# A hybrid decoder block in split fp32: reciprocal square roots seeded by ScalarE, output weights split where they are used, convolution sums kept in PSUM

## The chip, the core and the metric

One core of a Trainium2 chip runs the whole block. Its engines are TensorE (PE, matrix products), VectorE (DVE), ScalarE (ACT) and GpSimd (POOL); the SyncE queue (SP) issues most transfers. Each engine works off its own instructions strictly in order. The metric is the device time of one execution in microseconds, as a median over runs. The time also has a part before the first and after the last instruction; the span is what lies between those two.

## The reference

One layer, 1024 tokens, width 1024, 16 learned meta tokens put in front and cut off at the end; everything in fp32. With `rms` for a root-mean-square norm and `ln` for a layer norm it computes:

```
h   = concat(meta, x)                          # 1040 tokens
p   = rms(h, g_pre) @ w_in                     # 1024 x 2560: b, c, h, v, g (512 each)
y_a = b * conv3(c * h_)                        # causal depthwise, 3 taps
z   = conv31(v * sigmoid(g)) + bias            # causal depthwise, 31 taps
y   = concat(y_a, silu(ln(z)))                 # 512 + 512
h   = h + rms(y @ w_out, g_post)               # 1024 x 1024
f   = (silu(n @ w_gate) * (n @ w_up)) @ w_down # n = rms(h, g_ffn), inner width 2816
out = (h + rms(f, g_out))[16:]
```

Each `rms` and `ln` holds a reciprocal square root, of one number per token.

## The kernel before

**Split products.** Every fp32 operand of a product is kept as two rounded parts, hi and lo: a cast on ACT gives hi, a subtraction on DVE or GpSimd gives lo. `mm3` (L109 to L111) then issues three matmuls, hi\*hi, hi\*lo, lo\*hi, into one PSUM tile. That is why each product has three lines in the profile.

**Order.** Nothing is scheduled by a planner: the kernel is built with a manual schedule, and the order of the Python calls is the order of each engine's queue. An instruction that must wait holds up everything behind it on its engine.

**Stage 1, input projection.** The 2560 output columns are 20 *units* of 128: `g`, `v` (gate and value of the long convolution), `c`, `h`, `b` (short convolution), four of each. The units g0 and v0 are computed while x arrives. Then PE transposes and spreads the norm factors: `ss_x` (sums of squares, L271), `rsqrt_n` on DVE, `pb_x` (L286, in `start_g`) and ACT copies to `rB` (L289). Then 18 units follow in the order of `UNITS`: g1 v1 g2 v2 g3 v3, then c, h, b for each of the four column groups. While unit i is multiplied, `split_unit` prepares the weights of unit i+1 (hi on ACT, lo on GpSimd, L155), and `after[...]` deals with the result of unit i-1. `LEAD_IN` and `AT` say which convolution taps and which layer-norm steps are issued at which unit; `AT[(14, 1)]` is `ln_mean`, whose matmuls `pm` (L435) need all taps done.

**The long convolution.** The tokens are held in even and odd halves e and o. Three short convolutions give both outputs: a common one on o with summed weights (`ac`, 16 taps), one on d = e - o (`ae`, 16 taps) and one on e[1:] - o (`ao`, 15 taps). Each tap is one DVE instruction over 512 columns (L341). The accumulators lie in PSUM, but the first tap of each takes its start value from z in SBUF, and the common result goes back to z. The differences d and e[1:] - o are DVE instructions (L352, L353). For three of the four groups (of 128 channels) the first eight common taps are done on ACT and GpSimd (L335, L336), since `HEAD` is (1, 8, 8, 8).

**Output weights.** `pre_out` (called around the start of stage 1) loads each of 8 blocks of w_out, splits it (ACT L256, DVE L257) and writes hi and lo to DRAM. In stage 2 `next_o` loads hi and lo back from there on the GpSimd queue (L740), 18 times 512 KB each.

**Stage 2, output projection.** Token rows of 128 are taken in three groups, (0,1,2), (3,4,5), (6,7); `group` multiplies all 8 weight blocks for the rows of the group (`po`), `norms` makes the two norms, `turn` transposes the normed rows (`pt`) into the operands of the next stage.

**Stage 3, gate and up.** Seven products for each pair of column blocks (a Strassen form), 11 pairs; x and y are the PSUM tiles, B11, B21, T1, T2, ... the token-side operands, `op` the weight-side ones. `a_side` makes a weight-side operand, `split_lo` and `copy_hi` a token-side one.

**Stage 4, down projection.** Seven products again (qx, qy), with final norms row by row at the end of the program; L966 writes the output rows.

**`rsqrt_n`** (L113 to L132): on DVE alone. It forms v, makes a first guess with integer arithmetic on the bits of v (two instructions) and makes three Newton steps.

Of the kernel before, what the change touches and what calls it, by code (L numbers as in the profile page):

```python
# [15 lines left out]
P = 128  # L16
# [18 lines left out]
MAGIC = 1597463007.0  # L35
RSCALE = -1.0 / 8192.0
# [21 lines left out]
def hybrid_block(ctx: ExitStack, tc: tile.TileContext, xT, x, w_in, w_out, w_gate, w_up, w_down, par, g_post, g_ffn, g_out, out):  # L58
# [35 lines left out]
    pr = const.tile([P, lines(NPAR)], F32, name="pr")[:, :NPAR]  # L94
# [18 lines left out]
    def rsqrt_n(ss, inv_n, eps, n, name, more=None):  # L113

        v = sm.tile([P, 16], F32, tag="v", name=f"v_{name}")
        b = sm.tile([P, 16], I32, tag="b", name=f"b_{name}")
        s = sm.tile([P, 16], F32, tag="s", name=f"s_{name}")
        t = sm.tile([P, 16], F32, tag="tt", name=f"t_{name}")
        v, b, s, t = v[:, :n], b[:, :n], s[:, :n], t[:, :n]
        nc.vector.tensor_scalar(v, ss, inv_n, eps, op0=ALU.mult, op1=ALU.add)  # L120
        if more is not None:
            nc.vector.tensor_scalar(v, more, inv_n, v, op0=ALU.mult, op1=ALU.add)
        nc.vector.tensor_scalar(b, v.bitcast(I32), 1, None, op0=ALU.logical_shift_right)
        nc.vector.tensor_scalar(s.bitcast(I32), b, -1.0, MAGIC, op0=ALU.mult, op1=ALU.add)
        for k in (3.0, 12.0, 768.0):
            if n == 1:
                nc.vector.tensor_scalar(t, s, v, s, op0=ALU.mult, op1=ALU.mult)
            else:
                nc.vector.tensor_tensor(t, s, s, op=ALU.mult)
                nc.vector.tensor_tensor(t, t, v, op=ALU.mult)  # L130
            nc.vector.scalar_tensor_tensor(s, t, k, s, op0=ALU.subtract, op1=ALU.mult)
        return s  # L132


    nc.scalar.dma_start(pr, par)
    xhb = [xa.tile([P, 2 * TT], F32R, tag="x", name=f"xh{j}").rearrange("p (a b) -> p a b", a=2) for j in range(4)]
# [3 lines left out]
    wo = [dram.tile([P, 2, D], F32R, tag=f"wo{k}", name=f"wo{k}") for k in range(KD)]  # L140
# [88 lines left out]
    split_unit(UNITS[0])  # L229
    nc.vector.tensor_tensor(sa[0], sa[0], sa[1], op=ALU.add)  # L230

# [13 lines left out]
    ws_o = {}  # L245

    def load_raw_o(k):
        if k < KD:
            ws_o[k] = yap.tile([P, D], F32, tag="y", name=f"ws_o{k}")
            nc.sync.dma_start(ws_o[k], w_out[k])  # L250

    def pre_out(k):
        load_raw_o(k + 2)
        ws = ws_o.pop(k)
        h, l = (yap.tile([P, D], F32R, tag="y", name=f"{c}_o{k}") for c in ("wh", "wl"))
        nc.scalar.copy(h, ws)  # L256
# [18 lines left out]
    rx = rsqrt_n(sx[:, : NT + 1], 512.0 / D, RMS_EPS, NT + 1, "x")  # L275
    rB = row(gp, "rB", "rB", TT, bufs=1)
# [51 lines left out]
    def conv_head(a):  # L328

        ze, zo = halves_of(a)  # L330
        o = gpad[a][1]
        nc.scalar.activation(zo, o[:, :HALF], AF.Identity, scale=wc(a, 0), bias=pr[:, O_CBB + a : O_CBB + a + 1])
        for i in range(1, HEAD[a]):
            t = ct.tile([P, HALF], F32, tag="ct", name=f"ct{a}{i}")
            nc.scalar.activation(t, o[:, i : i + HALF], AF.Copy, scale=wc(a, i))  # L335
            nc.gpsimd.tensor_tensor(zo, zo, t, op=ALU.add)  # L336

    def taps(name, src, w, first, n, init, out):
        acc = aux.tile([P, 512], F32, tag="a", name=name)
        for i in range(first, n):  # L340
            nc.vector.scalar_tensor_tensor(out if i == n - 1 else acc, src[:, i : i + HALF], w(i), init if i == first else acc, op0=ALU.mult, op1=ALU.add)  # L341
            yield

    def common(a):
        ze, zo = halves_of(a)
        yield from taps(f"ac{a}", gpad[a][1], lambda i: wc(a, i), HEAD[a], NE, zo, zo)

    def even(a):
        e, o = gpad[a]
        ze, zo = halves_of(a)  # L350
        d = ct.tile([P, (G0 + TT) // 2], F32, tag="d", name=f"d{a}")
        nc.vector.tensor_tensor(d, e, o, op=ALU.subtract)  # L352
        nc.vector.tensor_tensor(o[:, :-1], e[:, 1:], o[:, :-1], op=ALU.subtract)  # L353
# [54 lines left out]
    def after_b(a):  # L408
# [4 lines left out]
        nc.scalar.copy(yh[a], cv[a])  # L413
        nc.vector.tensor_tensor(yl[a], cv[a], yh[a].bitcast(F32), op=ALU.subtract)
# [8 lines left out]
    def sums(srcs, outs):  # L423
        for q in range(3):
            for hf in range(2):
                nc.vector.tensor_tensor(outs[hf], srcs(hf, 0) if q == 0 else outs[hf], srcs(hf, q + 1), op=ALU.add)
# [787 lines left out]
```

## Time and profile before

| | |
|---|---|
| median of 3 runs | 1059.92 us (1058.63 to 1061.58) |
| the profiled execution | 1059.18 us |
| its span | 1057.2 us |
| mean granted TensorE clock | 0.972 |
| PE busy | 986.2 us, 93% of the span, 4643 matmuls |
| DVE, ACT, POOL busy | 773.9, 378.4, 296.3 us |

In the profile a row of the timeline reads: start, duration, engine, line of the kernel, operation, output from inputs, shape, and in brackets how long the engine was idle before and what released it. A windows row lists for a stretch of time the busy time of each engine with its number of instructions, then the granted clock of TensorE (1.00 is full speed), the busy share of the DMA engines and GB/s. A waits row gives what an engine waited for: in total, how many times, longest.

### The profile page before, as it was taken

What the parts mean: (1) busy time and instruction counts of PE and PEld (TensorE: products, weight loads), DVE (VectorE), ACT (ScalarE), POOL (GpSimd) and SP (SyncE); (2) the same over time, 40 slices, a digit from 0 to 9 for tenths busy, and PEclk for the clock granted to TensorE, in tenths of its full rate; (3) what the DMA queues carried; (4) which work ended last, traced back from release to release, by engine and by line L of the source; (5) the groups of instructions that cost most, each with busy time, mean ns of one, the idle gap of its engine ahead of it and who ended that gap; (6) DMA issues with size and microseconds to landing.
All of it is one profiled execution on the core that took longest, in us unless ns stands there. A gap on an engine that the chain in (4) does not pass through costs nothing.

```text
span 1057.2 us, 12732 instructions
## 1 busy us (share of the span) xinstructions
PE 986.2 (93%) x4643; PEld 839.9 (79%) x4643; DVE 773.9 (73%) x1087; ACT 378.4 (36%) x616; POOL 296.3 (28%) x267
## 2 busy tenths in 40 slices
PE   9599998879999797998999999999999899999994
PEld 8499998769787675876888888888888788888773
DVE  6689999997414558789888888888878343446667
ACT  7433331233413254333443433434334233322331
POOL 0247774443112100026134223313413522212110
PEclk9799998989999999999999999999999999999998
DMA  7851111001759552034634443353324989867765
GB/s 304 301 216 41 41 42 60 20 20 61 254 163 316 183 184 74 1 122 177 219 130 149 160 170 148 130 209 117 142 100 169 384 309 376 270 183 204 268 215 209
DMA packets 64909, 180.80 MB, mean 171 GB/s; under 512 B 6864, under 2 KB 7248, under 8 KB 64848
## 3 DMA queue, kind: packets, MB, share of 16 engines
q1 hardware_dynamic: 43344, 109.40, 28.2%
q0 software_dynamic: 16272, 59.25, 17.4%
q10 hardware_dynamic: 5232, 11.35, 3.0%
q8 instruction: 36, 0.59, 0.2%
q14 instruction: 25, 0.20, 0.1%
HBM read 122.83 MB, written 57.15 MB: 170 GB/s over the span
## 4 chain that ended last, share of the span: by engine, by line
PE 60%; DVE 26%; DMA 5%; ACT 4%; issue 4%; POOL 1%; SPq 0%; DVEq 0%; ACTq 0%; POOLq 0%
PE x L109 6%; PE x L111 6%; PE x L110 6%; PE y L109 5%; PE y L110 5%; PE y L111 5%; DVE ao L341 4%; DVE ae L341 4%; PE qx L110 3%; PE qx L109 3%; PE qx L111 3%; DVE ac L341 3%; PE qy L110 2%; PE qy L111 2%; PE qy L109 2%
## 5 line engine op out<-in xcount | busy, mean ns | idle before, releaser
L592 DVE TENSOR_TENSOR op<-u,op 128x512 fp32r<-128x512 f32 x154 | 142.9, 955 | 61.6 <-ACT op L605 61.6
L605 ACT CAST op<-u 128x512 fp32r<-128x512 f32 x154 | 90.7, 618 | 163.6 <-DVE u L592 153.6
L592 DVE TENSOR_TENSOR db<-wb,db 128x512 fp32r<-128x512 f32 x77 | 53.7, 701 | 93.2 <-ACT db L1015 92.9
L1015 ACT CAST db<-wb 128x512 fp32r<-128x512 f32 x77 | 47.0, 621 | 117.4 <-PE qx L111 55.2
L595 POOL TENSOR_TENSOR C<-C,C 128x512 f32<-128x512 f32 x11 | 15.4, 1400 | 246.8 <-ACT C L705 246.8
L109 PE MATMUL qx<-db,a 128*128 128x512 f32 x176 | 68.7, 390 | 3.2 <-DMA a<-gdA 3.2
L110 PE MATMUL qx<-db,a 128*128 128x512 f32 x176 | 68.7, 390 | 0.4 <-DVE db L592 0.3
L111 PE MATMUL qx<-db,a 128*128 128x512 f32 x176 | 68.5, 389 | 0.0
L595 POOL TENSOR_TENSOR U<-U,U 128x512 f32<-128x512 f32 x22 | 31.2, 1419 | 92.1 <-ACT U L705 83.4
L109 PE MATMUL qy<-db,a 128*128 128x512 f32 x132 | 51.5, 390 | 0.5 <-ACT db L1015 0.5
L110 PE MATMUL qy<-db,a 128*128 128x512 f32 x132 | 51.5, 390 | 0.3 <-DVE db L592 0.3
L111 PE MATMUL qy<-db,a 128*128 128x512 f32 x132 | 51.4, 389 | 0.0
L991 POOL DMA_DIRECT2D a<-gdS x44 | 23.3, 531 | 92.2 <-PE qy L111 47.2
L589 DVE TENSOR_TENSOR U<-y,U 128x512 f32<-128x512 f32 x66 | 42.7, 681 | 7.8 <-PE y L111 7.8
L341 DVE SCALAR_TENSOR_TENSOR ae<-d,pr,ae 128x512 f32<-128x512 f32 x56 | 41.8, 747 | 0.0
L109 PEld LDWEIGHTS qx<-db,a 128*128 128x128 f32 x176 | 33.0, 188 | 10.8 <-ACT U L705 3.6
L109 PE MATMUL y<-T2h,op 128*128 128x512 f32 x88 | 35.5, 403 | 5.6 <-DVE G L595 4.4
L592 DVE TENSOR_TENSOR u<-u,u 128x512 f32<-128x512 f32 x44 | 39.9, 907 | 0.8
L109 PE MATMUL x<-B21h,op 128*128 128x512 f32 x88 | 35.0, 398 | 5.3 <-ACT U L677 5.3
L109 PE MATMUL p_h<-xh,wh_h 128*128 128x342 f32 x96 | 32.8, 341 | 7.3 <-DVE cv L412 7.3
L110 PEld LDWEIGHTS qx<-db,a 128*128 128x128 f32 x176 | 33.0, 188 | 7.9 <-DVE db L592 1.2
L341 DVE SCALAR_TENSOR_TENSOR ao<-g,pr,ao 128x512 f32<-128x512 f32 x52 | 38.8, 747 | 0.0
(290 smaller groups left out, 3015.1 us busy)
## 6 DMA issues: line engine op xcount, KB each, us to landing
a<-gdS POOLq DMA_DIRECT2D x44, 512.0 KB, 4.7
a<-gdA POOLq DMA_DIRECT2D x33, 512.0 KB, 5.8
u<-w_gate_u SPq DMA_DIRECT2D x22, 512.0 KB, 5.4
u<-w_up_u SPq DMA_DIRECT2D x22, 512.0 KB, 5.9
gdS<-HI SPq DMA_DIRECT2D x44, 256.0 KB, 2.3
wh_o<-wo POOLq DMA_DIRECT2D x18, 512.0 KB, 5.8
wl_o<-wo POOLq DMA_DIRECT2D x18, 512.0 KB, 7.2
gdA<-HI SPq DMA_DIRECT2D x33, 256.0 KB, 2.0
```

The source lines that it names most:

```text
L109: nc.tensor.matmul(o, lh, rh, start=start, stop=False, skip_group_check=again)
L110: nc.tensor.matmul(o, lh, rl, start=False, stop=False, skip_group_check=again)
L111: nc.tensor.matmul(o, ll, rh, start=False, stop=stop, skip_group_check=again)
L341: nc.vector.scalar_tensor_tensor(out if i == n - 1 else acc, src[:, i : i + HALF], w(i), init if i == first else acc, op0=ALU.mult, op1=AL ...
L589: (eng or nc.vector).tensor_tensor(o, a, b, op=ALU.add)
L592: (eng or nc.vector).tensor_tensor(o, a, b, op=ALU.subtract)
L595: (eng or nc.vector).tensor_tensor(o, a, b, op=ALU.mult)
L605: nc.scalar.copy(t[:, 0, :], src)
L991: nc.gpsimd.dma_start(loads[n, j], gd[an][j])
L1015: nc.scalar.copy(t[:, 0, :], b)
```

## The change

1. `rsqrt_n` takes its first guess from ScalarE's function Abs_reciprocal_sqrt and makes one Newton step instead of three. ScalarE holds one table of functions at a time; `table(f)` issues a one-column instruction that loads a table ahead of its use. The program now loads seven tables; before it loaded three.
2. `pre_out` is gone. `load_o` loads the raw block of w_out on the SP queue and `split_o` splits it, once for each group of rows except that the blocks used last by one group are used first by the next: 14 loads of 512 KB. The first two blocks are split with GpSimd, the others with DVE. Blocks 3 and 4 are kept between the first groups.
3. In the start, lo of g1 and v1 is made by DVE, not GpSimd; all of v0 is multiplied ahead of `ss_x`; `start_g` is issued after two of the eight blocks of g1 instead of after one.
4. The convolution accumulators stay in PSUM from the first tap on: ACT writes the first common tap (or copies the eight) into PSUM tile `ac`, `ae` starts from `ac`, and the odd taps go on in `ac` itself. The differences are made by GpSimd. `value` writes even and odd tokens contiguously. The schedule of taps is new. The sums for the layer norm are kept in PSUM, and lo of a `b` unit is made three taps later.
5. Before stage 3: the hi half of B21 is made between the reciprocal square root and the residual sum, T2 is split in 128-column pieces, the weight sums of the product s = 4 are made earlier, T4's tiles are taken earlier, and in `a_side` both casts are issued ahead of both subtractions.

```diff
-    def rsqrt_n(ss, inv_n, eps, n, name, more=None):
-        nc.vector.tensor_scalar(v, ss, inv_n, eps, op0=ALU.mult, op1=ALU.add)
...
-        nc.vector.tensor_scalar(b, v.bitcast(I32), 1, None, op0=ALU.logical_shift_right)
-        nc.vector.tensor_scalar(s.bitcast(I32), b, -1.0, MAGIC, op0=ALU.mult, op1=ALU.add)
-        for k in (3.0, 12.0, 768.0):
...
+    def table(f):
+        nc.scalar.activation(eps[:, 2:3], eps[:, 0:1], f)
+
+    def rsqrt_n(ss, inv_n, e, n, name):
...
+        nc.scalar.activation(s, ss, AF.Abs_reciprocal_sqrt, scale=inv_n, bias=at)
+        nc.vector.tensor_scalar(v, ss, inv_n, e, op0=ALU.mult, op1=ALU.add)
...
+        nc.vector.scalar_tensor_tensor(r, t, 3.0, s, op0=ALU.subtract, op1=ALU.mult)
+        return r
...
+    def load_o(k):
+        raw_w["o", k] = wp.tile([P, D], F32, tag="ws", name=f"ws_o{k}")
+        nc.sync.dma_start(raw_w["o", k], w_out[k])
+
+    def split_o(k, eng=None):
...
+        nc.scalar.copy(wu[k][0], raw_w["o", k])
+        (eng or nc.vector).tensor_tensor(wu[k][1], raw_w["o", k], wu[k][0].bitcast(F32), op=ALU.subtract)
...
-    split_unit(UNITS[0])
     nc.vector.tensor_tensor(sa[0], sa[0], sa[1], op=ALU.add)
+    split_unit(UNITS[0], nc.vector)
...
+    mm_k(pu["v", 0], split_w["v", 0], KD - 1, 0, T3, 3)
     NT = SEQ // P
...
-    mm_k(pu["v", 0], split_w["v", 0], KD - 1, 0, T3, 3)
...
+    def differences(a):
+
+        e, o = gpad[a]
+        dd[a] = ct.tile([P, (G0 + TT) // 2], F32, tag="d", name=f"d{a}")
+        nc.gpsimd.tensor_tensor(dd[a], e, o, op=ALU.subtract)
+        nc.gpsimd.tensor_tensor(e[:, 1:], e[:, 1:], o[:, :-1], op=ALU.subtract)
...
+    def conv(a):
...
+        both = aux.tile([P, 512], F32, tag="a", name=f"ac{a}")
+        if HEAD[a] > 1:
+            nc.scalar.copy(both, zo)
+        else:
+            nc.scalar.activation(both, o[:, :HALF], AF.Identity, scale=wc(a, 0), bias=pr[:, O_CBB + a : O_CBB + a + 1])
+        yield from taps(o, lambda i: wc(a, i), HEAD[a], NE, both, both, both)
+        ae = aux.tile([P, 512], F32, tag="a", name=f"ae{a}")
+        yield from by_turns(taps(dd[a], lambda i: wb(a, 2 * i), 0, NE, both, ae, ze), taps(e[:, 1:], lambda i: wb(a, 2 * i + 1), 0, NE - 1, both, both, zo))
...
-    AT = {(0, 1): start_g, (14, 1): ln_mean, (15, 3): ln_var, (15, 7): ln_spread}
+    AT = {(0, 2): start_g, (14, 1): ln_mean, (15, 3): ln_var, (15, 7): ln_spread}
...
-    up, down_ = list(range(KD)), list(range(KD - 1, -1, -1))
+    up, middle = list(range(KD)), [5, 6, 7, 3, 4, 0, 1, 2]
...
-    s1, left = group((0, 1, 2), up, {})
+    s1, left = group((0, 1, 2), up, {0: ahead(3, 5), 1: ahead(4, 6), 2: ahead(5, 7), 3: ahead(6, 0), 4: ahead(7, 1), 6: ahead(None, 2)})
...
-    s1, left = group((3, 4, 5), down_, {4: turns(0, 1), 5: turns(2)})
+    s1, left = group((3, 4, 5), middle, {1: ahead(0, 5), 2: ahead(1, 6), 3: ahead(2, 7), 4: turns(0, 1), 5: turns(2)})
...
-    hn = norms((6, 7), left, s1, hs, between)
+    hn = norms((6, 7), left, s1, hs, between, lambda: copy_hi(X[2], r21))
+    table(AF.Silu)
```

The change moves instructions at three places of which the prediction speaks. The first is DVE's queue at the norm of x, where the convolution begins. The names are: `v_x`, `b_x`, `s_x`, `t_x` the steps of the reciprocal square root, `wl_o` lo of an output weight, `sg` the gate of unit g0, `rB` the spread norm. Before (left out in the middle are the second step of the guess and the nine of the three Newton steps):

```order
L273 COPY sx<-ss_x 128x8
L274 COPY sx<-ss_x 16x1
L120 TENSOR_SCALAR v_x<-sx 128x9
L123 TENSOR_SCALAR b_x<-v_x 128x9
...
L257 TENSOR_TENSOR wl_o_438<-ws_o_358,wh_o_437 128x1024
L257 TENSOR_TENSOR wl_o_446<-ws_o_366,wh_o_445 128x1024
L257 TENSOR_TENSOR wl_o_454<-ws_o_435,wh_o_453 128x1024
L257 TENSOR_TENSOR wl_o_462<-ws_o_443,wh_o_461 128x1024
L477 TENSOR_TENSOR sg_423<-sg_423,rB 128x1044
```

And now:

```order
L241 TENSOR_TENSOR sa_134<-sa_134,sa_135 128x1040
L153 TENSOR_TENSOR wl_g_218<-ws_g_186,wh_g_217 128x1024
L272 COPY sx<-ss_x 128x8
L273 COPY sx<-ss_x 16x1
L124 TENSOR_SCALAR v_x<-sx 128x9
L128 TENSOR_TENSOR tt_x<-s_x 128x9
L129 TENSOR_TENSOR tt_x<-tt_x,v_x 128x9
L130 SCALAR_TENSOR_TENSOR r_x<-tt_x,s_x 128x9
L153 TENSOR_TENSOR wl_v_399<-ws_v_188,wh_v_398 128x1024
L479 TENSOR_TENSOR sg_377<-sg_377,rB 128x1044
```

The chain has four DVE instructions where it had twelve, its guess `s_x` comes from ACT, and the splits of output weights that stood between it and the gate are gone; lo of g1 and of v1 has come to DVE.

The second place is the end of the common taps of the first convolution group on DVE. `ac`, `ae`, `ao` are accumulators in PSUM, `g` holds e and o, `d` is their difference, z lies in SBUF, `pr` and `wsum` are the weights. Before:

```order
L341 SCALAR_TENSOR_TENSOR ac_585<-g_508,wsum,ac_585 128x512 x5
L341 SCALAR_TENSOR_TENSOR z_427<-g_508,wsum,ac_585 128x512
L352 TENSOR_TENSOR d_707<-g_508 128x527
L353 TENSOR_TENSOR g_508<-g_508 128x526
L341 SCALAR_TENSOR_TENSOR ae_710<-d_707,pr,z_427 128x512
L341 SCALAR_TENSOR_TENSOR ao_712<-g_508,pr,z_427 128x512
L341 SCALAR_TENSOR_TENSOR ae_710<-d_707,pr,ae_710 128x512
```

And now:

```order
L344 SCALAR_TENSOR_TENSOR ac_512<-g_442,wsum,ac_512 128x512 x13
L310 TENSOR_TENSOR g_606<-p_v_527,sg_508 128x2x174 x3
L344 SCALAR_TENSOR_TENSOR ac_512<-g_442,wsum,ac_512 128x512 x2
L344 SCALAR_TENSOR_TENSOR ae_616<-d_445,pr,ac_512 128x512
L344 SCALAR_TENSOR_TENSOR ac_512<-g_442,pr,ac_512 128x512
L344 SCALAR_TENSOR_TENSOR ae_616<-d_445,pr,ae_616 128x512
```

The two differences have left DVE, and no tap but the last of each output touches z.

The third place is ACT's queue at the start of the output projection. `yh` and `ybh` are hi parts of the operands, `wh_o` and `w_o` of the weight blocks, `gB_post` and `gB_ffn` gains. Before:

```order
L413 CAST yh_2255<-cv_2193 128x1024
L473 ACTIVATE gB_post<-gB_post 128x1024
L473 ACTIVATE gB_ffn<-gB_ffn 128x1024
L527 CAST ybh_2282<-z_427 128x2x512 x2
L527 CAST ybh_2288<-z_428 128x2x512 x2
```

And now:

```order
L406 CAST yh_2192<-cv_2124 128x1024
L542 CAST ybh_2219<-z_396 128x2x512
L167 CAST wh_o_2223<-ws_o_2190 128x1024
...
L542 CAST ybh_2231<-z_397 128x2x512 x2
L475 ACTIVATE gB_post<-gB_post 128x1024
L475 ACTIVATE gB_ffn<-gB_ffn 128x1024
L117 ACT_TABLE_LOAD
L117 ACTIVATE pr<-pr 128x1
L167 CAST w_o_2217<-ws_o_2227 128x1024
L167 CAST w_o_2218<-ws_o_2325 128x1024
```

Left out is a second `ybh` cast of z_396. The hi cast of block 3 (`w_o_2217`) now stands behind eight instructions that follow `yh` of the last unit.

More of the change, by code (lines that the diff above doesn't have):

```diff
@@ L519, in hybrid_block @@
     ps2 = pa.enter_context(tc.tile_pool(name="ps2", bufs=6, space=PSUM, reuse_waits="tile"))
+    held = [xg.tile([P, 2, D], F32R, tag="x", name=f"w_o{k}") for k in (3, 4)]
     for a in range(4):
@@ L768, in group, with ahead, f @@
         return s1, {i: leave_psum(i, pm[i], s1, q) for q, i in enumerate(grp)}
-    up, down_ = list(range(KD)), list(range(KD - 1, -1, -1))
-    for q in range(3):
-        next_o()
+    def ahead(k=None, n=None):
+        def f():
+            if k is not None:
+                split_o(k)
+            if n is not None:
+                load_o(n)
+        return f
+    up, middle = list(range(KD)), [5, 6, 7, 3, 4, 0, 1, 2]
+    load_o(4)
     hs = {i: residual_x(i) for i in (0, 1, 2)}
     pairs = {j: Pair(j) for j in range(3)}
-    pairs[0].load(0)
-    pairs[1].load(0, (0,))
-    s1, left = group((0, 1, 2), up, {})
+    s1, left = group((0, 1, 2), up, {0: ahead(3, 5), 1: ahead(4, 6), 2: ahead(5, 7), 3: ahead(6, 0), 4: ahead(7, 1), 6: ahead(None, 2)})
     B11 = [blocks(big(f"B11{j}", pool=bp)) for j in "hl"]
-    for q, t in ((0, 0), (1, 1), (0, 1), (1, 0)):
-        raw[q, t] = blocks(big(f"raw{q}{t}", F32))
+    for q in range(2):
+        raw[q, 0] = blocks(big(f"raw{q}0", F32))
     hn = norms((0, 1, 2), left, s1, hs)
@@ L825, in a_side, with pairs_load @@
             pairs[j + 1] = Pair(j + 1)
-        made[s] = [pairs[j].a_side(n, m, places[m] if places else None) for m in range(2)]
+        src = sums.pop(s, None) or [pairs[j].a_side(n, m) for m in range(2)]
+        t = [operand_hi(src[m], f"{n}_{j}{m}", places[m] if places else None) for m in range(2)]
+        for m in range(2):
+            sub(t[m][:, 1, :], src[m], t[m][:, 0, :].bitcast(F32))
+        made[s] = t
+    def pairs_load():
+        split_o(7)
+        pairs[1].load(0, (0,))
     def early():
+        for q in range(2):
+            raw[q, 1] = blocks(big(f"raw{q}1", F32))
         turns(3, 4, 5)()
         pairs[1].load(0, (1,))
-        t1_sum(0)
-        t1_sum(1)
+        for i in range(2):
+            t1_sum(i)
         a_side(0)
@@ L854, in hybrid_block @@
     st = ctx.enter_context(tc.tile_pool(name="st", bufs=11, reuse_waits="tile"))
+    X[6] = pair("T2", (rp, rp))
     a_side(3)
-    for i in range(2):
-        t2_sum(i)
-    def t2():
-        X[6] = pair("T2", (rp, rp))
-        copy_hi(X[6], T2r)
-        split_lo(X[6], T2r)
+    for f in (t2_sum, t2_hi, t2_lo):
+        for i in range(2):
+            f(i)
     def t1():
@@ L914, in hybrid_block @@
             turns(6, 7)()
+            sums[4] = [pairs[0].a_side(6, m) for m in range(2)]
         if s in (14, 15):
```

230 lines of the change are left out of this document (113 added, 117 removed).

## The prediction

> **What bounds the kernel now.** I read the page first, then PE's waits, then the stretches of time one by one, then single rows where two engines meet.
>
> ```profile
> PE 986.2 (93%) x4643; PEld 839.9 (79%) x4643; DVE 773.9 (73%) x1087; ACT 378.4 (36%) x616; POOL 296.3 (28%) x267
> PE pb_x L286 <- ACT rB L289: 10.6, 1, 10.6
> PE p_h L109 <- DVE cv L412: 7.3, 2, 3.9
> PE pm L435 <- DVE zs L426: 6.2, 1, 6.2
> PE x L109 <- ACT U L677: 5.3, 2, 4.1
> PE po L110 <- DMA wl_o<-wo: 3.9, 4, 1.8
> PE po L109 <- DMA wh_o<-wo: 3.5, 1, 3.5
> ```
>
> PE is busy 93% of the span, so a gain can only come from its 71 us of idle time and from the time in which its clock is low. A gain on DVE, ACT or POOL counts only where PE waits for it. The waits are few and long, and lie before 435 us. The windows show stretch by stretch what each engine did (length, then the busy time of PE, its weight loads, DVE, ACT and POOL, then the granted clock, the DMA share and GB/s).
>
> ```profile
> 62.40:119.60 57.20, 57.20 (x361) 57.20 (x360) 53.55 (x66) 19.87 (x25) 39.25 (x24) 1.00 0.17 61
> 119.60:142.10 22.50, 22.50 (x145) 22.50 (x144) 22.40 (x30) 8.46 (x11) 15.30 (x12) 1.00 0.11 38
> 200.00:230.00 30.00, 19.95 (x111) 18.94 (x110) 28.83 (x41) 3.85 (x4) 9.86 (x5) 0.87 0.11 36
> 62.40:279.10 216.70, 203.08 (x1157) 191.80 (x1156) 194.44 (x241) 65.10 (x75) 106.95 (x58) 0.96 0.16 54
> 279.10:386.90 107.80, 97.03 (x433) 77.64 (x432) 46.05 (x93) 34.23 (x68) 16.93 (x32) 0.97 0.69 237
> 386.90:432.70 45.80, 38.07 (x161) 30.19 (x161) 37.05 (x68) 20.76 (x36) 0.00 (x0) 0.93 0.20 69
> 500.00:820.00 320.00, 320.00 (x1413) 265.03 (x1413) 268.96 (x346) 128.53 (x231) 87.72 (x57) 1.00 0.42 153
> ```
>
> From 500 to 820 us PE never stops at full clock: nothing is to be had there. The projection (62 to 279) falls behind only after 142 us, where DVE is full (28.83 of 30) and PE waits for it. The start and the stages from 279 to 433 have waits of their own. The change touches these.
>
> **Part A, the start (−15.9).** PE reaches the end of g1 at 62.33 us.
>
> ```profile
> 31.26 2.08 PE L271 MATMUL ss_x<-ones,sa 128*128 128x1 f32 x18 [1.66 <-DVE sa L230]
> 48.13 1.04 ACT L256 CAST wh_o<-ws_o 128x1024 fp32r<-128x1024 f32 x1 [3.31 <-DMA ws_o<-w_out_u]
> 49.31 1.11 PE L286 MATMUL pb_x<-ident,s_x 128*128 128x128 f32 x4 [10.63 <-ACT rB L289]
> 62.33 0.32 PE L109 MATMUL p_v<-xh,wh_v 128*128 128x348 f32 x1
> ```
>
> The 10.63 us are ACT's: its copy to rB stood behind casts of output weights that waited for their loads. `pre_out` is gone, so are these casts. The last nine matmuls of v0 now come ahead of `ss_x`. Nine at the unit's spacing (57.20 / 360 = 0.159) fill 1.43 of the 1.66 us of waiting; the sum that PE waited for also comes earlier, since the subtraction that GpSimd ran beside it has gone behind it on DVE. From 31.1, then: `ss_x` 2.1, 72 matmuls of g1 11.44, `pb_x` 1.9 with its short wait: 46.4, so −15.9. The norm factors must be ready after two blocks of g1, at 36.0; the shortened chain ends near 35. If the thin matmuls of `ss_x` lower the clock once more, up to 1.5 comes back.
>
> **Part B, the projection (−20.2).** The floor of the 216.7 us: five g and v units 57.2, eight c and h units 22.50 / 2 = 11.25 each, four b units at 48 times 0.23 (14 intervals below) = 11.05, and the layer norm's matmuls.
>
> ```profile
> 275.67 0.39 PE L109 MATMUL p_b<-xh,wh_b 128*128 128x512 f32 x1
> 278.89 0.40 PE L111 MATMUL p_b<-xh,wl_b 128*128 128x512 f32 x1
> 229.35 3.46 PE L435 MATMUL pm<-zs,ones 128*128 128x512 f32 x4 [6.15 <-DVE zs L426]
> L446 PE MATMUL pst<-ones,sq 128*128 128x1 f32 x16 | 1.8, 245 | 0.0
> L454 PE MATMUL pv<-ident,s_ln 128*128 128x128 f32 x8 | 1.1, 279 | 0.1
> ```
>
> `pm` needs about 1.3 less at full clock (an estimate from its slow stretch), so the three are 5.1. Together 57.2 + 90.0 + 44.2 + 5.1 = 196.5. The 20.2 above it are 13.5 of waits (7.3 + 6.2) and 6.7 of slow clock behind them. They vanish if DVE is in time. What DVE loses:
>
> ```profile
> 65.62 2.34 DVE L341 SCALAR_TENSOR_TENSOR ac<-g,wsum,z 128x512 f32<-128x512 f32 x1 [1.85 <-ACT z L332]
> L341 DVE SCALAR_TENSOR_TENSOR ae<-d,pr,z 128x512 f32<-128x512 f32 x4 | 9.3, 2337 | 0.0
> L341 DVE SCALAR_TENSOR_TENSOR ae<-d,pr,ae 128x512 f32<-128x512 f32 x56 | 41.8, 747 | 0.0
> L353 DVE TENSOR_TENSOR g<-g 128x526 f32<-128x526 f32 x4 | 8.9, 2221 | 0.2
> L352 DVE TENSOR_TENSOR d<-g 128x527 f32<-128x527 f32 x4 | 6.9, 1718 | 0.0
> 197.51 2.74 POOL L406 TENSOR_TENSOR cv<-cv,rB 128x1024 f32<-128x1024 f32 x1
> 197.92 2.89 DVE L341 SCALAR_TENSOR_TENSOR ae<-d,pr,z 128x512 f32<-128x512 f32 x1
> ```
>
> A first tap with both inputs in SBUF takes 2337 ns on the mean, one on a PSUM accumulator 747. The last two rows say why: the tap at 197.92 takes 2.89 while GpSimd works beside it. Taps with one input in PSUM are not held up so. So the eight first taps of `ae` and `ao` shrink by 8 times 1.59 = 12.7, and the differences, 15.8, leave DVE. DVE's stretch from the first tap (65.62) to the matmul `pm` (229.35) is 163.7 us; without these 28.5 it is 135.2. It begins 3.2 us after g1's end: the gate of g1, its sigmoid and ACT's first tap come ahead, as they do now. So it begins at 49.6 and ends near 185; I give it 6 either way, for the first taps of `ac`, which are shorter too, and for what GpSimd's new work may hold up. In a projection without waits `pm` is due at 46.4 + 57.2 + 67.5 + 22.1 + 1.4 = 194.6 (five units, six, two and a block of the next). The margin is 4 to 16, so I take the whole 20.2. The other bound is that none of it comes; it is a rival below.
>
> **Part C, output projection (−11.8).** 384 `po` matmuls at 0.2267 (18 intervals below) are 87.0, six rows transposed at 1.1 are 6.6: 93.6 of 107.8.
>
> ```profile
> 599.35 0.39 PE L109 MATMUL x<-B11h,op 128*128 128x512 f32 x1
> 603.43 0.39 PE L109 MATMUL x<-B11h,op 128*128 128x512 f32 x1
> 376.92 1.03 PE L573 MATMUL pt<-ident,hn 128*128 128x128 f32 x8
> 51.07 1.28 ACT L478 ACT_TABLE_LOAD   x1
> ```
>
> The reloads from DRAM (7.4 us of waits) are replaced by half the traffic and by 14 casts on ACT (1.04 in the row at 48.13) and as many subtractions, most on DVE (2.36 for two of this shape in part D), engines that were busy 34 and 46 of 107.8. The tightest is block 3: its cast stands behind eight ACT instructions of about 1.1, a table load of 1.28 and the one behind it; with its own cast that is some 11.3, then 1.2 for lo: 12.5 after the last unit, while PE asks for it after 54 matmuls, at 12.2. I keep 2.4 of stalls (blocks 3 and 5, transposes): 96.0.
>
> The Trainium skill ("ScalarE: Activation LUTs", What ACT_TABLE_LOAD costs) counts a drain with each switch, some 2.7 us in all. That speaks against four more loads. The row at 51.07 shows 1.28. By the page block 3 would be 1.4 later, and the total 1003; no run here yet shows a load with work behind it that PE waits for.
>
> **Part D, start of gate and up (−8.4).** Six products of 24 matmuls 32.6 and two transposed rows 2.2 are 34.8 of 45.8.
>
> ```profile
> 388.72 0.17 DVE L120 TENSOR_SCALAR v_pm<-pm 128x2 f32<-128x2 f32 x1
> 390.90 0.16 DVE L131 SCALAR_TENSOR_TENSOR s_pm<-t_pm,s_pm 128x2 f32<-128x2 f32 x1
> 413.70 2.36 DVE L592 TENSOR_TENSOR T2l<-T2r,T2h 128x1024 fp32r<-128x1024 f32 x2
> ```
>
> One root costs 2.35 on DVE, and two stand on this path; four instructions and ACT's guess come to about 1.1, which saves 2.4. T2, sum and lo, stood last on DVE's list; half of it is now made before the last rows arrive. I leave 2.6 of waits: 37.4. If only the roots help, −2.4.
>
> **Part E, the tail (−2.4).** Two chains of this kind lie behind the last matmul:
>
> ```profile
> 1043.60 0.15 DVE L120 TENSOR_SCALAR v_out<-tot 128x1 f32<-128x1 f32 x1
> 1045.48 0.16 DVE L131 SCALAR_TENSOR_TENSOR s_out<-t_out,s_out 128x1 f32<-128x1 f32 x1
> ```
>
> 2.04 each becomes about 0.85, bounds 0.5 and 1.2 saved per chain. The other table loads stand where ACT has idle time (36% busy) and cost nothing; uncovered they are 1.5 each. The 5.3 for U are not touched.
>
> Sum: −15.9 − 20.2 − 11.8 − 8.4 − 2.4 = −58.7, from the profiled execution's 1059.18 (0.74 under the median): 1000.5. Several margins are about 1 us; with 1.5 for them, **1002**.
>
> **The rivals.** *GpSimd is late.* It gains eight differences and keeps its adds and splits, in one queue:
>
> ```profile
> 77.84 10.88 POOL L336 TENSOR_TENSOR z<-z,ct 128x512 f32<-128x512 f32 x7 [7.58 <-ACT ct L335]
> ```
>
> Before c0, from the values of v2 at about 84, come two differences (1.4 each, half of the 128x1024 row at 197.51), seven adds 10.9 and the split 2.7: it is done at 100 to 102, and PE asks at 103.6. If the differences take 2.2 as on DVE and the rest runs slower beside it, lo of c0 and of later units comes 2 to 3 us late, four or five times: about +10, **1012**. *The splits are late in the output projection* because raw loads or ACT's queue hold them, and D gives only its roots: +9, **1010**. Against it: DMA was 0.69 busy there with twice the traffic. *DVE still sets the pace:* if held-up instructions stay as many, its 163.7 us run from 49.6 to 213, 19 late, and the gain of part B is gone: **1021**. The 747 ns of taps on PSUM speak against it.
>
> *Slower:* a denser stream lowers the granted clock. It has its place in the long middle, 990 us of matmuls, where each 0.01 costs about 10; from a mean of 0.915 on the gain is gone, at 0.90 the time is **1075**. Against it stand 320 us without a pause at 1.00.
>
> The Trainium skill ("TensorE: Matmul & The Clock Gate", Part 1) says the opposite of that rival: idleness of about 3.4 us halves the clock. The slow stretches above follow waits, which agrees.
>
> **How the numbers follow.** Forecast 1002 (990 to 1008): 0.55. GpSimd late: 0.18. Splits late: 0.13. DVE still bound (1021), or only part A (1043): 0.09. Slower: 0.02. Better, without my 1.5 + 2.4 + 2.6 and with the waits for U and the slow clock behind them gone (986 to 990): 0.03. The range 986 to 1029 takes in all but the ends. A measurement tells 0.3% (3.2 us) from no change: faster 0.95, same 0.02, slower 0.03.
>
> **What would show it.** Right: g1 ends near 46, `pm` waits under 1 us and the clock is 1.00 from 140 to 230; the first `po` matmul starts near 243, the first x product near 339; no wait for DMA at `po`; the roots take about 1 us. Wrong: waits of PE for `wl_c` or `wl_h` (GpSimd), for `wh_o`, `w_o` (splits), for `zs` or `cv` (DVE), or a clock below 0.97 with few waits.

## The result and the profile after

The changed kernel takes 994.95 us (median of four runs, 994.0 to 995.7) where the kernel before takes 1060.24; the ratio is 0.9384, 95% interval 0.9368 to 0.9401. Its profiled execution took 994.89 us, with a span of 993.1 us and a mean clock of 0.995 (before: 0.972). The prediction was 1002, in a range of 986 to 1029.

From the page of the changed kernel the busy times and the clock in 40 slices (in tenths of full speed), and the four longest of PE's waits:

```profile
PE 967.6 (97%) x4643; PEld 829.3 (84%) x4643; DVE 723.3 (73%) x997; ACT 398.4 (40%) x650; POOL 279.9 (28%) x239
PEclk9999999999999999999999999999999999999998
PE x L108 <- ACT U L698: 3.9, 2, 2.7
PE pt L595 <- ACT raw L597: 2.9, 4, 1.2
PE qx L108 <- DMA a<-gdA: 2.4, 1, 2.4
PE y L108 <- DVE G L617: 1.7, 1, 1.7
```

PE issues the same 4643 matmuls, but idles 25.5 us instead of 71. The waits for `rB`, `zs`, `wl_o` and `wh_o` are gone from the list, and those for `cv` in the projection. PE's busy time has also fallen, by 18.6 us: matmuls at low clock count as longer ones (0.63 us instead of 0.39 in rows shown at the end). The windows of the changed kernel, by the stages of the prediction, show how little is left:

```profile
45.70:242.20 196.50, 196.50 (x1157) 187.15 (x1156) 160.66 (x225) 70.64 (x84) 114.44 (x64) 1.00 0.16 53
242.20:339.00 96.80, 93.44 (x434) 77.01 (x433) 54.47 (x73) 48.69 (x86) 0.00 (x0) 1.00 0.42 149
339.00:377.40 38.40, 35.26 (x162) 28.65 (x161) 33.92 (x54) 23.01 (x42) 0.00 (x0) 1.00 0.24 83
```

In the window of the projection PE is busy 196.50 of 196.50 us at full clock. Between the first matmuls of two stages the projection takes 196.7, where the prediction had worked out a floor of 196.5. Laid out by the first matmul of each stage:

| stretch | before, us | after, us | change | forecast |
|---|---|---|---|---|
| to the first matmul of v1 | 62.3 | 45.5 | −16.8 | −15.9 |
| projection, to the first `po` | 216.8 | 196.7 | −20.1 | −20.2 |
| output projection, to the first x | 107.8 | 96.8 | −11.0 | −11.8 |
| first x to the first product with T1 | 45.8 | 38.4 | −7.4 | −8.4 |
| T1 to the last matmul | 610.4 | 604.8 | −5.6 | 0 |
| last matmul to the end | 14.1 | 10.9 | −3.2 | −2.4 |

The whole is −64.1 of span. Five rows came within 1 us of the forecast; the row from T1 on was not foreseen. That row is the least firm: in the profiles of nine runs below whose order from x on is the changed kernel's, or differs from it only in ways that turned out to cost nothing, this stretch takes 602.2 to 605.7 us, so its gain is between about 5 and 8.

### The profile page after: what moved, and what is told of

It is laid out like the page before. It is cut to its first block, busy times and chain, and to the rows that moved or that the text cites. A ratio compares the mean times of both kernels' runs of the same rounds, so it can differ in the third digit from the quotient of the medians.

```text
span 993.1 us, 12601 instructions
## 1 busy us (share of the span) xinstructions
PE 967.6 (97%) x4643; PEld 829.3 (84%) x4643; DVE 723.3 (73%) x997; ACT 398.4 (40%) x650; POOL 279.9 (28%) x239
## 4 chain that ended last, share of the span: by engine, by line
PE 85%; DVE 8%; issue 2%; ACT 2%; DMA 1%; ACTq 0%; DVEq 0%; POOL 0%; SPq 0%; POOLq 0%
PE x L108 6%; PE x L109 6%; PE x L110 6%; PE y L108 5%; PE y L109 5%; PE y L110 5%; PE qx L109 4%; PE qx L108 4%; PE qx L110 4%; PE po L108 3%; PE po L110 3%; PE po L109 3%; PE qy L109 3%; PE qy L110 3%; PE qy L108 3%
## 5 line engine op out<-in xcount | busy, mean ns | idle before, releaser
L614 DVE TENSOR_TENSOR op<-u,op 128x512 fp32r<-128x512 f32 x154 | 145.8, 980 | 24.5 <-ACT op L627 23.4
L617 POOL TENSOR_TENSOR C<-C,C 128x512 f32<-128x512 f32 x11 | 17.6, 1598 | 325.2 <-ACT C L726 175.6
L344 DVE SCALAR_TENSOR_TENSOR ac<-g,pr,ac 128x512 f32<-128x512 f32 x56 | 41.9, 748 | 0.0
L108 PEld LDWEIGHTS qx<-db,a 128*128 128x128 f32 x176 | 33.0, 188 | 9.9 <-issue 2.8
L109 PEld LDWEIGHTS qx<-db,a 128*128 128x128 f32 x176 | 33.0, 188 | 7.4 <-DVE db L614 0.6
L110 PEld LDWEIGHTS qx<-db,a 128*128 128x128 f32 x176 | 33.0, 188 | 6.9
```

Of the source, the lines that this page charges most:

```text
L108: nc.tensor.matmul(o, lh, rh, start=start, stop=False, skip_group_check=again)
L109: nc.tensor.matmul(o, lh, rl, start=False, stop=False, skip_group_check=again)
L110: nc.tensor.matmul(o, ll, rh, start=False, stop=stop, skip_group_check=again)
L614: (eng or nc.vector).tensor_tensor(o, a, b, op=ALU.subtract)
L617: (eng or nc.vector).tensor_tensor(o, a, b, op=ALU.mult)
```

## The experiments

Each one is the changed kernel with one part set back or moved, run beside the kernel before. "Pm" is the time at which PE reaches the layer norm's first matmul (194.3 in the changed kernel).

| run | us | ratio to before, 95% |
|---|---|---|
| the changed kernel | 994.95 | 0.9384 (0.9368 to 0.9401) |
| differences on DVE | 993.65 | 0.9364 (0.9346 to 0.9382) |
| start values in SBUF | 993.32 | 0.9362 (0.9341 to 0.9383) |
| both | 998.38 | 0.9417 (0.9391 to 0.9442) |
| the whole convolution as before | 1013.39 | 0.9552 (0.9536 to 0.9569) |
| output weights by way of DRAM | 1022.42 | 0.9634 (0.9611 to 0.9658) |
| the start's splits and order as before | 999.84 | 0.9426 (0.9403 to 0.9450) |
| old root | 1006.22 | 0.9492 (0.9465 to 0.9519) |
| tables loaded at their use | 994.64 | 0.9383 (0.9356 to 0.9410) |
| order ahead of T1 as before | 1008.56 | 0.9512 (0.9494 to 0.9531) |
| cast and subtraction by turns | 994.83 | 0.9376 (0.9353 to 0.9400) |
| T4's tiles late | 994.57 | 0.9379 (0.9362 to 0.9396) |
| copy of U first | 994.10 | 0.9375 (0.9356 to 0.9393) |

### The long convolution: three runs on two suspects, and a fourth

Differences back on DVE, just ahead of the even taps:

```diff
-        nc.gpsimd.tensor_tensor(dd[a], e, o, op=ALU.subtract)
-        nc.gpsimd.tensor_tensor(e[:, 1:], e[:, 1:], o[:, :-1], op=ALU.subtract)
+        nc.vector.tensor_tensor(dd[a], e, o, op=ALU.subtract)
+        nc.vector.tensor_tensor(e[:, 1:], e[:, 1:], o[:, :-1], op=ALU.subtract)
...
+        differences_now(a)
```

> The changed kernel with the eight differences back on VectorE, made just ahead of the even taps. Theory (slack): in the changed kernel VectorE ended the sums for pm at 183.0 us and TensorE asked at 194.3, so it has about 11 us to spare; the differences cost 5.6 (0.7 each, undisturbed) to 15.8 (as before), so the time rises by 0 to 5, to 995 to 1000, with a wait at pm of 0 to 5. Rival (the differences on GpSimd are themselves the cure): the whole of part B goes, +16 and more, 1011 or above.

Start values from z in SBUF:

```diff
-            nc.scalar.copy(both, zo)
+            pass
...
-        yield from taps(o, lambda i: wc(a, i), HEAD[a], NE, both, both, both)
+        yield from taps(o, lambda i: wc(a, i), HEAD[a], NE, zo, both, zo)
...
-        yield from by_turns(taps(dd[a], lambda i: wb(a, 2 * i), 0, NE, both, ae, ze), taps(e[:, 1:], lambda i: wb(a, 2 * i + 1), 0, NE - 1, both, both, zo))
+        yield from by_turns(taps(dd[a], lambda i: wb(a, 2 * i), 0, NE, zo, ae, ze), taps(e[:, 1:], lambda i: wb(a, 2 * i + 1), 0, NE - 1, zo, both, zo))
```

> The changed kernel with the start values of the taps read from SBUF again (z), and the common sum written back there; differences stay on GpSimd. Theory (first taps with two SBUF inputs are held up by GpSimd): twelve first taps rise from 0.75 to 1.7 to 2.3 us, 12 to 16 in all, against 11 of slack: +0 to +5, 995 to 1000; the rows of the first taps show 2 to 3 us while GpSimd works. Rival (the hold-up came only from VectorE's own differences or was a matter of the order): first taps stay at about 0.75 and the time at 995.

Both together:

> Both: differences on VectorE and start values in SBUF. Theory (slack used up): 28 to 32 us more on VectorE against 11 of slack, so pm and the short convolution make TensorE wait about 17 to 21, with some slow clock behind: 1012 to 1021, far more than the sum of the two single steps. Rival (no slack, the costs add): the sum of the two single steps.

Each step alone costs nothing (993.65 and 993.32). Both cost 3.4 us (four runs, 997.7 to 1002.5). The slack is real, and it can be read in the timeline of DVE in the changed kernel, where the sums end at 183.0 and the next row waits for PE:

```profile
179.32 1.30 DVE L424 TENSOR_TENSOR zp<-z 128x512 f32<-128x512 f32 x2
...
181.72 1.28 DVE L424 TENSOR_TENSOR zs<-zp,z 128x512 f32<-128x512 f32 x2
193.21 1.23 DVE L392 TENSOR_TENSOR cs<-p_h,cs 128x1026 f32<-128x1026 f32 x1 [10.21 <-PE p_h L110]
```

With either step alone the sums end at 193.3 and 193.2, so DVE is about 10 us later, within the 11 of slack. With both they end at 199.0, 16 later, and the projection takes 202.1 instead of 196.7. PE does not wait at `pm` even then; it waits earlier, twice for DVE and once for GpSimd:

```profile
PE p_c L108 <- DVE cs L396: 1.5, 1, 1.5
PE p_c L108 <- DVE sg L296: 1.2, 1, 1.2
PE p_b L110 <- POOL wl_b L153: 1.1, 1, 1.1
```

But 12 to 21 had been expected of the two together, with 28 to 32 us more on DVE. The theory had a size wrong: the hold-up did not come back at its old rate. With the start values in SBUF, five of the twelve first taps took 1.4 to 2.8 us and the seven others 0.74 to 0.84. So the whole convolution was set back, with its schedule of taps:

```diff
-    taps_ = {1: 13, 3: 14, 5: 14, 7: 16, 9: 10, 10: 16, 11: 14}
-    LEAD_IN = {i: (lambda n=n: tap(n)) for i, n in taps_.items()}
...
+    LEAD_IN = {1: some(lambda: conv_head(0), lambda: tap(9)), 2: some(lambda: conv_head(1), lambda: tap(10)), 3: lambda: tap(14), 4: some(lambda: conv_head(2), lambda: tap(13)), 5: lambda: tap(14), 6: some(lambda: conv_head(3), lambda: tap(12)), 7: lambda: tap(16), 8: lambda: tap(13), 9: lambda: tap(12), 10: lambda: tap(15), 11: lambda: tap(12), 12: lambda: tap(12), 13: some(lambda: tap(40), ln_sum), 16: some(ln_apply), 17: some(gains)}
```

> The changed kernel with the whole long convolution as before (differences on VectorE, start values from z, the old schedule of taps with two common sums by turns, lo of b at once); only the contiguous g and the layer norm's sums in PSUM stay. Theory (the schedule carries what differences and start values together did not: the two alone cost 16 us of VectorE, the kernel before lost 28 at the same places because GpSimd worked just then): first taps are back at 2.3 us, pm is asked at 194 and comes 10 to 16 late: 1008 to 1015. Rival (the schedule does not matter): as with the two alone, 998 to 1000.

It came out at 1013.39, 18.4 above the changed kernel, with the old waits back:

```profile
PE p_h L108 <- DVE cv L406: 8.3, 2, 6.6
PE pm L434 <- DVE zs L424: 5.7, 1, 5.7
```

The same instructions in the two runs, grouped by form, first the old schedule:

```profile
L335 DVE SCALAR_TENSOR_TENSOR ae<-d,pr,z 128x512 f32<-128x512 f32 x4 | 9.4, 2340 | 0.0
L347 DVE TENSOR_TENSOR g<-g 128x526 f32<-128x526 f32 x4 | 8.9, 2221 | 0.2
L346 DVE TENSOR_TENSOR d<-g 128x527 f32<-128x527 f32 x4 | 6.8, 1700 | 0.0
```

and with both steps undone but the new schedule kept:

```profile
L343 DVE TENSOR_TENSOR g<-g 128x526 f32<-128x526 f32 x4 | 5.9, 1470 | 0.1
L342 DVE TENSOR_TENSOR d<-g 128x527 f32<-128x527 f32 x4 | 4.9, 1217 | 0.0
L347 DVE SCALAR_TENSOR_TENSOR ae<-d,pr,z 128x512 f32<-128x512 f32 x4 | 4.0, 1011 | 0.0
```

The same first tap takes 2340 ns on the mean in the one and 1011 in the other. I laid each of the sixteen differences and first taps of `ae` and the odd chain against GpSimd's rows in both timelines. With the old schedule GpSimd worked beside all sixteen, and fifteen of them took 1.6 to 2.9 us; the other, beside 0.33 us of GpSimd, took 0.69. With the new one nine had no GpSimd work beside them and took 0.70 to 0.75; the seven others took 0.7 to 2.8. So part 4 gains at this place in two ways: held-up operations are removed, and the new schedule places such operations where GpSimd is idle. The new schedule with neither of the two moves nearly suffices (998.38); the two moves with the old schedule were not tried. What the old schedule sets back, the places of the taps, the order of the chains and lo of a `b` unit at once, was not separated either.

### The output weights

The weights split at the start, written to DRAM and loaded back, everything else as changed:

```diff
-            split_o(0, nc.gpsimd)
...
+    for k in range(2):
+        load_raw_o(k)
+    for k in range(2):
+        pre_out(k)
...
+            if s or grp[0] == 0:
+                next_o()
```

> The changed kernel with the output weights split once at the start, written to DRAM and loaded back, as before; all else as changed. Theory: the wait for pb_x at the start returns with its slow clock (+12 to +16, g1 ends near 60) and the output projection returns to about 107 (+10): 1017 to 1021. Rival (the start was won by the lo parts on VectorE and the shorter root): the start keeps at least half of its gain, g1 ends before 54, and the time is under 1013.

1022.42, 27.5 more: of it 12.7 before pm (g1 ends at 58.2) and 14.1 in the output projection, which takes 110.9. The old wait is back (10.50, where it was 10.63), and so is its cause, ACT at a cast that waits for a load:

```profile
46.17 1.04 ACT L258 CAST wh_o<-ws_o 128x1024 fp32r<-128x1024 f32 x1 [2.94 <-DMA ws_o<-w_out_u]
47.35 1.12 PE L297 MATMUL pb_x<-ident,r_x 128*128 128x128 f32 x4 [10.50 <-ACT rB L300]
PE po L109 <- DMA wl_o<-wo: 8.8, 5, 2.3
```

The rival, that the lo parts on DVE and the shorter root won the start, falls: g1 ends well behind 54. The rest of the start was tried by itself:

```diff
+    split_unit(UNITS[0])
     nc.vector.tensor_tensor(sa[0], sa[0], sa[1], op=ALU.add)
-    split_unit(UNITS[0], nc.vector)
...
-    mm_k(pu["v", 0], split_w["v", 0], KD - 1, 0, T3, 3)
...
+    mm_k(pu["v", 0], split_w["v", 0], KD - 1, 0, T3, 3)
...
-    AT = {(0, 2): start_g, (14, 1): ln_mean, (15, 3): ln_var, (15, 7): ln_spread}
+    AT = {(0, 1): start_g, (14, 1): ln_mean, (15, 3): ln_var, (15, 7): ln_spread}
```

Lo of g1 is then made by GpSimd ahead of the sum of squares, and lo of v1 by GpSimd too; the last block of v0 stands behind `ss_x` again.

> The changed kernel with the start as before, save for the output weights: lo of g1 and v1 on GpSimd, the last block of v0 behind ss_x, the spread after one block of g1. Theory (the 10.6 us were ACT's casts of output weights, and the bounce run has returned 12.6 of the 16.8): the rest, 2 to 5, returns, as a wait for the sum of squares (1.7) and some slow clock; g1 ends near 48 to 50 and the time is 997 to 1000. Rival (the casts alone made the start slow): within 1 of 995.

999.84, as expected; pm is 4.6 later. Two rows of PE show why more than the wait is lost:

```profile
31.24 2.08 PE L262 MATMUL ss_x<-ones,sa 128*128 128x1 f32 x18 [1.45 <-DVE sa L242]
35.48 0.49 PE L108 MATMUL p_g<-xh,wh_g 128*128 128x348 f32 x1
```

After 1.45 us of idling and 2.08 of one-column matmuls, the 348-column matmuls take 0.49 instead of 0.32 from 34.0 to 37.2 us. In the changed kernel `ss_x` follows without a wait, and the clock stays at 1.00. 12.7 and 4.6 make 17.3 against the 16.8 that the start gained. The first `ss_x` alone lies between 30.7 and 33.0 in the profiles of these runs, so within that the start is accounted for. How the 4.6 divide among the three things set back was not separated.

### The root and its tables

The old root on DVE, without the loads of its table:

```diff
-        nc.scalar.activation(s, ss, AF.Abs_reciprocal_sqrt, scale=inv_n, bias=at)
...
+        nc.vector.tensor_scalar(s.bitcast(I32), b, -1.0, MAGIC, op0=ALU.mult, op1=ALU.add)
+        for k in (3.0, 12.0, 768.0):
```

> The changed kernel with the old reciprocal square root (VectorE alone, three Newton steps) and without the loads of its table. Theory: two roots on the way to the first products of gate and up cost 1.2 each, the two behind the last matmul 1.1 each, and the start keeps its time because the factors are needed only after two blocks of g1: +4 to +6, 999 to 1001. Rival (the added table loads eat the gain): within 2 of 995.

1006.22, 11.3 more, twice what was expected. In the profiled execution (1009.47, the longest of the four) 3.3 lie in the tail (14.2 instead of 10.9), 4.8 between x and T1, 2.0 behind T1, and 4.3 in the output projection, which had not been thought of: there the long chains stand on DVE ahead of lo parts of weights, and PE waits.

```profile
PE pt L604 <- ACT raw L606: 4.3, 4, 1.6
PE po L111 <- DVE wl_o L177: 2.3, 1, 2.3
```

The start keeps its time, as expected (pm at 194.6).

Every table loaded where it is first used (`table` does nothing):

> The changed kernel without the early loads: each table is loaded where its first function needs it. Theory: a load of 1.28 stands on the path where TensorE waits for the root or the function: at the norm of x, at the norms ahead of the first products and at the tail's first root; +1 to +4, 996 to 999. Rival (loads are hidden anyway): within 1 of 995. By 2.7 us a load, as the Trainium skill counts a switch (ScalarE: Activation LUTs, What ACT_TABLE_LOAD costs), it would be +3 to +8.

No change, 994.64. Each stage up to T1 and the tail have the length that they had. First ACT in the changed kernel, then with late loads:

```profile
33.59 1.28 ACT L117 ACT_TABLE_LOAD   x1
34.89 0.20 ACT L117 ACTIVATE pr<-pr 128x1 f32<-128x1 f32 x1
```

```profile
33.37 1.28 ACT L124 ACT_TABLE_LOAD   x1 [1.15 <-DVE sx L274]
34.67 0.30 ACT L124 ACTIVATE s_x<-sx,pr 128x9 f32<-128x9 f32 x1
```

The norm of x does come 1.4 later, at 35.6 instead of 34.2, but PE asks for it only after two blocks of g1, at 36.0 and 35.8. The changed kernel makes seven loads, the one with late loads eight, each of 1.28; neither where they stand nor the one more makes a difference. The Trainium skill ("ScalarE: Activation LUTs", What ACT_TABLE_LOAD costs) counts 2.66 us for a switch, a drain of 1.38 in it; here the next instruction begins 1.30 after the load began in both rows, and the measurement decides.

### The order around the first products

Everything around the first products of gate and up as before (hi of B21, T2, the sums of product 4, T4's tiles, cast and subtraction by turns):

```diff
-    hn = norms((6, 7), left, s1, hs, between, lambda: copy_hi(X[2], r21))
+    copy_hi(X[2], r21)
+    hn = norms((6, 7), left, s1, hs, between)
...
-    for f in (t2_sum, t2_hi, t2_lo):
...
+    for i in range(2):
+        t2_sum(i)
...
+    def t2():
+        X[6] = pair("T2", (rp, rp))
```

> The changed kernel with the whole order around the first products of gate and up as before (hi half of B21 ahead of the norms, T2 made in one piece late, sums of product 4 late, T4's tiles taken late, cast and subtraction by turns). Theory: the first products take 43 to 46 instead of 38.4, less 2.4 that the shorter roots keep, and the stretch from T1 to the last matmul gets back its 5.6: +9 to +12, 1004 to 1007. Rival (the roots gave this stage's gain): +3 to +5.

1008.56, 13.6 more. The first products take 45.8, exactly as before, although the roots are short. So the roots' 2.4 are worth nothing here without the new order. PE's old waits for G (4.5 instead of 1.7) and, later, for T4's `op` are back:

```profile
PE y L108 <- DVE G L617: 4.5, 1, 4.5
PE x L108 <- ACT op L627: 1.5, 1, 1.5
```

The timeline of DVE shows where the roots' 2.4 go, first in the kernel before, then in this run:

```profile
403.46 1.29 DVE L592 TENSOR_TENSOR T2r<-raw,raw 128x512 f32<-128x512 f32 x2
404.66 0.68 DVE L592 TENSOR_TENSOR raw<-raw,raw 128x512 f32<-128x512 f32 x1
```

```profile
353.05 1.29 DVE L614 TENSOR_TENSOR T2r<-raw,raw 128x512 f32<-128x512 f32 x2
356.33 0.69 DVE L614 TENSOR_TENSOR raw<-raw,raw 128x512 f32<-128x512 f32 x1 [2.00 <-ACT raw L597]
```

DVE arrives 2 us earlier and waits 2.00 us for the last transposed rows, which PE makes only after the product before. Counted from the first x product, the step (`raw`) begins at 17.7 us in the one and at 17.6 in the other. The new order fills this gap with the second weight sums and half of T2.

The stretch from T1 to the last matmul also goes back, from 604.8 to 611.3. Two parts of the change were therefore tried for it alone. Cast and subtraction by turns:

```diff
-        t = [operand_hi(src[m], f"{n}_{j}{m}", places[m] if places else None) for m in range(2)]
+        t = []
         for m in range(2):
+            t.append(operand_hi(src[m], f"{n}_{j}{m}", places[m] if places else None))
             sub(t[m][:, 1, :], src[m], t[m][:, 0, :].bitcast(F32))
```

> The changed kernel with the operands of gate and up made one after the other again (cast, subtraction, cast, subtraction). Theory: the unforeseen gain from 430 us on (5.6 us) comes in part from VectorE no longer waiting for each cast; the wait for the copy of U goes from 2.7 back towards 4.1 and one for op returns: +1 to +4, 996 to 999. Rival (it comes from T4's tiles alone): no change.

And T4's tiles late:

```diff
-        T4.append(blocks(big("T4l")))
...
-        T4.append(blocks(big("T4h")))
...
-        l, h = T4
-        X[4] = h, l
         halves(sub, r21, r21, T2r)
+        X[4] = pair("T4", (None, None))
```

> The changed kernel with T4's two tiles taken where they were before, in t4. Theory (the 5.6 us from T1 to the last matmul were won because VectorE's backlog of the first products was gone, not by the tiles): no change, 994 to 996. Rival (the tiles came free late): the wait at T4's first product (1.5 and 0.7) and slow clock behind it return, +2 to +5, 997 to 1000.

Neither changes anything (994.83, 994.57). With the whole order as before, T4's first product waits for its operand again (1.47 and 0.74, where it was 1.49 and 0.74) and some slow clock follows. So the gain from T1 on goes with the order. That it belongs to the steps ahead of T1 (T2 in pieces, the early sums or hi of B21) is likely, not shown: the two parts that cost nothing singly were not undone together, and the steps ahead of T1 not by themselves.

### A wait that moves

The longest wait left is that for the copy of U. Ahead of it ACT makes three casts into HI, of which two wait for HI's transfers, 0.42 and 0.65 us. The copy was put first:

```diff
-        if s in (14, 15):
+        if s == 14:
             pairs[first_splits[s][0]].split(*first_splits[s][1:])
         results.pop(s - 1)()
+        if s == 15:
+            pairs[first_splits[s][0]].split(*first_splits[s][1:])
```

> The changed kernel with one line moved: at product 15 of gate and up, the copy of U out of PSUM on ACT is issued ahead of the casts into HI instead of behind them. Theory (TensorE's longest wait that is left, 2.7 us for the copy of U, comes from ACT standing at casts that wait for HI's transfers): that wait falls under 0.5 and the slow clock behind it (1.3) goes: -2 to -4, 991 to 993. Rival (ACT is late there because its own work comes late from VectorE): no change.

The wait of 2.7 is gone and so is the slow clock behind it, but a new wait, the first row below, stands in its place a product later; the second row, for U, was there before:

```profile
PE y L110 <- DVE op L614: 1.6, 1, 1.6
PE x L108 <- ACT U L698: 1.2, 1, 1.2
```

994.10 is not told apart from 994.95. That the casts ahead of the copy made this wait is shown; a gain is not.

## Why the prediction came out as it did

**Right, step by step.** Part A: the 10.6 us were ACT's queue of output-weight casts; the run by way of DRAM returned the wait. (The terms of this part add up to 46.5, not 46.4; PE reached v1 at 45.5.) The 1.5 that thin matmuls might cost did not come: `ss_x` no longer follows a wait, and in the run where it does, matmuls of 0.32 us take 0.49. Part B: the floor of 196.5 and DVE's end ("near 185", measured 183.0) held; so did the margin for `pm`. GpSimd, the first rival, was in time: lo of c0 was done at 99.4 where 100 to 102 had been estimated, with 1.34 and 1.12 us for two differences, and PE's first matmul of c0 stands at 102.8. Part C: PE waits for no weights.

**Luck, part C.** Block 3 was a near thing. Its lo was ready at 255.43, 13.2 behind the last unit's end where 12.5 had been worked out, and PE came for it 0.2 later:

```profile
254.20 1.23 DVE L168 TENSOR_TENSOR w_o<-ws_o,w_o 128x1024 fp32r<-128x1024 f32 x1 [2.53 <-ACT w_o L167]
255.64 0.40 PE L109 MATMUL po<-w_o,yh 128*128 128x512 f32 x1
```

PE was itself 0.69 late there, since a `po` matmul at 243.7 had waited that long for `cv`. So no wait shows, but without that earlier one PE would have come before the lo was ready.

**Right in its sum, wrong in what earns it, part B.** The sixteen instructions took 34.5 us before and the eight that are left take 6.0, so the 28.5 did leave DVE, and its end came out. But I put them down to the two moves. Undone together in the new schedule, the sixteen take 18.8, so the moves save 12.8 of the 28.5: the length of such an instruction depends on what GpSimd does beside it, and the new schedule had moved that. The schedule, of which the prediction said nothing, carries the rest.

**Sizes.** In part C I kept 2.4 of stalls, for blocks 3 and 5 and the transposes; the weights cost none, but the transposes kept all four of their waits, 2.9 as before, and one of 0.7 for `cv` stayed. In part E one chain was worth 2.05, not 1.2: it now ends, at 982.33, before the last matmul's result, and hides behind it altogether.

**Wrong, part D.** "If only the roots help, −2.4": with short roots and the old order the stretch is 45.8, so nothing. The step that failed is "two stand on this path". They stand on DVE's path, but the next step waits for rows that PE's own order brings. The 7.4 come from the order and the roots together: undoing the one costs 7.4, the other 4.8.

**Wrong, the stretch after T1.** "The 5.3 for U are not touched", and nothing was put down for 610 us: it fell by 5.6. The step that failed is a reading: "the waits are few and long, and lie before 435 us". Behind 433 PE idled 10.9 us before (599.55 busy of 610.40), among them 4.1 for U at 494, 3.2 for `a` at 831 and 1.5 and 0.7 at T4's first product. T4's wait has gone, with its slow clock; the other two fell to 2.7 and 2.4. T4's wait comes back when the order around the first products is set back, and I had costed that order only up to T1. The wait for U does not: it was 2.8 in that run. Why it fell stays open.

**The last rival.** The denser stream lowered no clock; the mean rose from 0.972 to 0.995.

## What to carry to other kernels

Work out the floor of a stage from its matmuls and their spacing, and compare it with the measured length: where nothing else bounds it, the whole difference, waits and the slow clock behind them, is the price of being late. In the projection all of it came back once DVE was in time, and 5.4 of it was lost again when DVE ended 16 us later. Cost a shortened chain at the next thing that it meets: between the first x and T1 the short root was worth nothing in the old order, and 4.8 us in the new one. And undo parts together as well as singly: two steps that each cost nothing can share one slack.

## What the runs showed of the hardware

In the convolution a DVE instruction with both inputs in SBUF took 0.69 to 0.76 us for about 512 columns with GpSimd idle and up to 2.9 with GpSimd at work; a tap with one input in PSUM took 0.72 to 0.77 in either case. Not every overlap costs DVE: in the run with start values in SBUF four first taps took 0.74 to 0.84 beside GpSimd. In each of these GpSimd's next instruction began behind the tap and took 1.6 to 1.7, where the same instructions take 1.1 to 1.3 in the changed kernel. It looks as if the one that begins second is held up; no run was made to test it. The sums for the layer norm show the hold-up of DVE too: with both inputs in SBUF the first two took 1.30 together in the changed kernel, and 5.02 in the run with both steps undone, where GpSimd worked beside them for 4.5:

```profile
191.63 5.02 DVE L428 TENSOR_TENSOR zp<-z 128x512 f32<-128x512 f32 x2
```

The clock falls after some short pauses and not after others. In the changed kernel a wait of 2.73 us was followed by six matmuls at about half speed, one of 2.38 by none. The same wait of 1.84 us before the same matmul was followed by a slow stretch in the run with start values in SBUF, and by none in the run with both steps undone. The first four rows are of the changed kernel, the next two of the one run and the last two of the other:

```profile
434.64 0.79 PE L108 MATMUL x<-B21h,op 128*128 128x512 f32 x1 [2.73 <-ACT U L698]
435.66 0.63 PE L110 MATMUL x<-B21h,op 128*128 128x512 f32 x1
770.56 0.47 PE L108 MATMUL qx<-db,a 128*128 128x512 f32 x1 [2.38 <-DMA a<-gdA]
770.87 0.39 PE L109 MATMUL qx<-db,a 128*128 128x512 f32 x1
```

```profile
769.58 0.47 PE L108 MATMUL qx<-db,a 128*128 128x512 f32 x1 [1.84 <-DMA a<-gdA]
771.14 0.63 PE L108 MATMUL qx<-db,a 128*128 128x512 f32 x1
```

```profile
773.30 0.47 PE L108 MATMUL qx<-db,a 128*128 128x512 f32 x1 [1.84 <-DMA a<-gdA]
774.53 0.39 PE L110 MATMUL qx<-db,a 128*128 128x512 f32 x1
```

The Trainium skill ("TensorE: Matmul & The Clock Gate", Part 1) names an idle window of about 3.4 us. Here 1.84 was enough once, and in the run with the old order around the first products a wait of 3.52 was followed by no slow matmul, so the length of a pause did not by itself decide. What does, no run here shows, nor how one-column matmuls count.
